# One Strassen level in the output and the down projection of a decoder layer, token parts through DRAM

## The chip, the cores and the metric

One core of a Trainium2 chip. The metric is the device time of one launch in microseconds (us), as the median of timed runs. The engines work side by side, each through its own queue in order: PE (TensorE, matmuls; PEld is its weight load), DVE (VectorE, elementwise), ACT (ScalarE, copies and activations), POOL (GpSimd), and SP, from which all DMAs of this kernel are issued (SPq is its queue). Matmuls write PSUM, eight banks of 128 x 512 floats; the rest lies in SBUF, 128 partitions.

## The reference

One decoder layer on x of 512 tokens x 2048 features, all in float32:

```
h = rms(x) * norm_mix_pre                 proj = h @ w_in
y_a = hgrn2(q, f, i, g) @ w_up_a          y_b = fox(q, k, v, f) @ w_up_b
m = sigmoid(g_a) * y_a + sigmoid(g_b) * y_b
x = x + rms(m @ w_o) * norm_mix_post                       # w_o: 2048 x 2048
h = rms(x) * norm_ffn_pre
gate, up = split(h @ w_ffn_in)                             # 2048 x 2*5632
x = x + rms((silu(gate) * up) @ w_ffn_down) * norm_ffn_post  # 5632 x 2048
```

The two products that the change touches are m @ w_o (the output projection, tiles `wo`) and act @ w_ffn_down (the down projection, tiles `dn`).

## The kernel before

**Products in three passes.** Every float32 operand is split into two parts of the type float32r: ACT copies it to that type (the high part), DVE subtracts the copy from the original (the low part). A product is then three matmuls into one bank: low x high, high x low, high x high (`mm3`, `mm3t`). So each weight tile of 128 x 1024 needs one ACT copy (L135) and one DVE subtraction (L136); `make_w` does it for three tiles ahead.

**Stages.** The input projection with both mixers comes first, with features on the partitions and 512 tokens in the free dimension. `merge` (L500) forms the two gates and adds the branches; its last call leaves the 16 tiles of m in SBUF, feature-major. Then m is split, and `rows_product` makes the output projection: tokens are the stationary side (128 of them), weights move through 512 columns at a time. It runs over two halves of 1024 columns. In each half 8 banks hold 4 token tiles x 2 column tiles, and the loop goes over the 16 k tiles:

```
for i in range(n_k - tail):
    w, a = next_w(), lhs(half, ks[i])
    for t in range(NT):
        block(t, a, w, i == 0, i == n_k - 1)
```

In the second half the last TAIL = 4 k tiles are done bank by bank, so that the token tiles are finished one after another. `wo_done` (L676) takes a finished bank: DVE multiplies it with norm_mix_post (L678), ACT squares and sums it (L679); with the last of a token tile the norm follows (sum, POOL's power, `wor`), the residual is added (L688), stored to DRAM (`x1d`), squared again and scaled (L696). `take_h(th)` transposes a half of 256 tokens on PE (`hp`, L724), scales it out of PSUM (L729) and makes the parts that the next stage wants.

**Gate and up projection (`f..p`, L151 to L153).** This stage is already done with one Strassen level in seven products: p1 to p7 with the token parts h11, h12, s1 to s4, h22 (`hx`) and the weights' parts `fia` to `fid`. The first five blocks do p1 and p2 first (NJ0), which need the first token half alone. Its results go to DRAM, `actd`.

**Down projection.** `rows_product` again, over 44 k tiles in each of two column halves; the activations come back from `actd` (256 KB tiles, L866) and are split for each half (L175, L176). `down_done` scales with norm_ffn_post, and with the last of a token tile makes the norm, adds `x1r` (x1 read back) and stores the output (L901, L902).

**Order.** The Tile framework puts the instructions into each engine's queue, by program order and by what it takes to be ready, and sets all waits. `tc.issue_after(loads[-1].ins)` queues DMAs behind the last weight load. A tile's buffer comes free when its last reader is done; the next tile of its tag waits for that.

## Time and profile before

| | us |
|---|---|
| median of 3 timed runs | 2881.95 (2881.37 to 2884.63) |
| the profiled execution | 2883.7 |
| its span, first to last instruction | 2882.0 |
| output projection | 1284.4 to 1465.2 |
| gate and up projection | 1491.8 to 2388 |
| down projection | 2393 to 2873.7 |

The profile is of one execution. The span is what its instructions cover; the 1.7 us beside it lie around them. A row of a view gives an engine's busy time in a stretch; what an engine waited for stands in brackets in a timeline.

### The profile page before, as it was taken

How to read it: one execution, taken by the hardware profiler on the slowest of the kernel's cores; microseconds unless marked ns; L12 is line 12 of the kernel's file. 1: busy time of each engine (PE TensorE's matmuls, PEld its weight loads, DVE VectorE, ACT ScalarE, POOL GpSimd, SP SyncE). 2: the span in 40 equal slices, each digit the busy share in tenths (PEclk: the TensorE clock that was granted, in tenths of full speed). 3: DMA queues.
4: the chain of work that ended last, by engine and by line, in shares of the span. 5: the costliest groups of instructions: out<-in, count | busy, mean ns of one | idle time of the engine just before them, and what ended most of it. 6: DMA issues, size and time to landing. Idle time of an engine off the chain costs nothing.

```text
span 2882.0 us, 39661 instructions
## 1 busy us (share of the span) xinstructions
PE 2829.7 (98%) x16320; PEld 2495.4 (87%) x16320; DVE 1624.4 (56%) x2311; ACT 1079.1 (37%) x1406; POOL 35.0 (1%) x75
## 2 busy tenths in 40 slices
PE   9999999999999999999969999999999999999998
PEld 7788888888888888888869999999999997888887
DVE  4776665333344433352279888888888885334234
ACT  4454544222233342232264444444444443224222
POOL 1000000000000000000000000000000000000000
PEclk9999999999999999999989999999999999999999
DMA  6323333333333333352344434344343438225353
GB/s 161 101 68 88 81 82 84 99 95 95 98 90 88 88 90 97 96 190 95 96 131 138 130 111 128 111 121 118 114 125 110 129 96 288 95 95 171 132 183 114
DMA packets 465143, 332.93 MB, mean 116 GB/s; under 512 B 12809, under 2 KB 422458, under 8 KB 464962
## 3 DMA queue, kind: packets, MB, share of 16 engines
q1 hardware_dynamic: 464962, 330.39, 39.0%
q8 instruction: 128, 2.10, 0.3%
q14 instruction: 53, 0.43, 0.0%
HBM read 310.40 MB, written 19.94 MB: 115 GB/s over the span
## 4 chain that ended last, share of the span: by engine, by line
PE 96%; DVE 2%; ACT 1%; issue 1%; DMA 0%; POOL 0%; SPq 0%; DVEq 0%; POOLq 0%; ACTq 0%
PE dn L157 6%; PE dn L158 6%; PE dn L159 5%; PE b L151 3%; PE b L153 3%; PE b L152 3%; PE p L151 3%; PE p L152 3%; PE p L153 3%; PE ga L153 2%; PE ga L152 2%; PE gb L151 2%; PE gb L153 2%; PE gb L152 2%; PE ga L151 2%; PE wo L157 2%
## 5 line engine op out<-in xcount | busy, mean ns | idle before, releaser
L136 DVE TENSOR_TENSOR wl<-wr,wh 128x1024 fp32r<-128x1024 f32 (+1 forms) x334 | 404.8, 1212 | 528.3 <-ACT wh L135 527.2
L135 ACT ACTIVATE wh<-wr 128x1024 fp32r<-128x1024 f32 (+1 forms) x334 | 349.8, 1048 | 925.9 <-PE dn L159 155.1
L810 DVE TENSOR_TENSOR fl<-fia,fh 128x1024 fp32r<-128x1024 f32 x88 | 107.7, 1224 | 79.3 <-ACT fh L809 79.3
L809 ACT ACTIVATE fh<-fid 128x1024 fp32r<-128x1024 f32 x88 | 93.4, 1062 | 112.4 <-DVE fid L799 33.1
L809 ACT ACTIVATE fh<-fic 128x1024 fp32r<-128x1024 f32 x88 | 93.4, 1062 | 111.1 <-DVE fic L805 102.7
L810 DVE TENSOR_TENSOR fl<-fic,fh 128x1024 fp32r<-128x1024 f32 x88 | 107.8, 1225 | 34.9 <-ACT fh L809 34.7
L809 ACT ACTIVATE fh<-fia 128x1024 fp32r<-128x1024 f32 x88 | 93.4, 1062 | 90.4 <-DVE fia L803 47.6
L810 DVE TENSOR_TENSOR fl<-fid,fh 128x1024 fp32r<-128x1024 f32 x88 | 107.1, 1217 | 3.5 <-ACT fh L809 3.5
L853 ACT ACTIVATE t<-g 128x512 f32<-128x512 f32 x44 | 27.8, 632 | 95.9 <-DVE g L852 95.9
L809 ACT ACTIVATE fh<-fib 128x1024 fp32r<-128x1024 f32 x44 | 46.7, 1061 | 32.3 <-DVE fib L801 28.5
L805 DVE TENSOR_TENSOR fic<-fia,fic 128x1024 f32<-128x1024 f32 x44 | 53.8, 1224 | 1.3
L799 DVE TENSOR_TENSOR fid<-fid,fib 128x1024 f32<-128x1024 f32 x44 | 53.7, 1220 | 0.1
L801 DVE TENSOR_TENSOR fib<-fib,fia 128x1024 f32<-128x1024 f32 x44 | 53.6, 1218 | 0.0
L810 DVE TENSOR_TENSOR fl<-fib,fh 128x1024 fp32r<-128x1024 f32 x44 | 53.6, 1217 | 0.0
L803 DVE TENSOR_TENSOR fia<-fia,fid 128x1024 f32<-128x1024 f32 x44 | 53.5, 1217 | 0.0
L513 DVE TENSOR_TENSOR sga<-ya,sga 128x512 f32<-128x512 f32 x16 | 11.1, 692 | 52.8 <-PE ya L153 52.8
L506 DVE TENSOR_TENSOR sga<-ga,rb 128x512 f32<-128x512 f32 x16 | 11.1, 692 | 52.0 <-PE ga L153 52.0
L513 DVE TENSOR_TENSOR sgb<-yb,sgb 128x512 f32<-128x512 f32 x16 | 11.1, 692 | 47.7 <-PE yb L153 47.7
L724 PE MATMUL hp<-ident,mo 128*128 128x128 f32 x64 | 12.2, 353 | 21.6 <-DVE mo L696 21.6
L724 PEld LDWEIGHTS hp<-ident,mo 128*128 128x128 f32 x64 | 10.0, 183 | 24.3 <-issue 15.7
L855 DVE TENSOR_TENSOR g<-g,u 128x512 f32<-128x512 f32 x44 | 30.1, 684 | 0.0
L854 DVE TENSOR_TENSOR g<-g,t 128x512 f32<-128x512 f32 x44 | 30.1, 684 | 0.0
(8848 smaller groups left out, 9493.0 us busy)
## 6 DMA issues: line engine op xcount, KB each, us to landing
wr<-in_w_in_dram SPq DMA_DIRECT2D x166, 512.0 KB, 3.9
wr<-in_w_ffn_down_dram SPq DMA_DIRECT2D x88, 512.0 KB, 3.9
fic<-in_w_ffn_in_dram SPq DMA_DIRECT2D x49, 512.0 KB, 4.0
fia<-in_w_ffn_in_dram SPq DMA_DIRECT2D x49, 512.0 KB, 3.9
fid<-in_w_ffn_in_dram SPq DMA_DIRECT2D x44, 512.0 KB, 5.1
fib<-in_w_ffn_in_dram SPq DMA_DIRECT2D x44, 512.0 KB, 4.0
act<-actd SPq DMA_DIRECT2D x88, 256.0 KB, 5.9
wr<-in_w_o_dram SPq DMA_DIRECT2D x32, 512.0 KB, 3.8
```

The costliest lines, as they stand in the source:

```text
L135: hi = nc.scalar.activation(wh[:, 0:width], raw[:, 0:width], AF.Copy)
L136: lo = nc.vector.tensor_tensor(wl[:, 0:width], raw[:, 0:width], wh[:, 0:width].bitcast(F32), ALU.subtract)
L151: nc.tensor.matmul(ps, lhsT=wh, rhs=xl, start=first, stop=False)
L152: nc.tensor.matmul(ps, lhsT=wh, rhs=xh, start=False, stop=False)
L153: nc.tensor.matmul(ps, lhsT=wl, rhs=xh, start=False, stop=last)
L157: nc.tensor.matmul(ps, lhsT=xl, rhs=wh, start=first, stop=False)
L158: nc.tensor.matmul(ps, lhsT=xh, rhs=wl, start=False, stop=False)
L159: nc.tensor.matmul(ps, lhsT=xh, rhs=wh, start=False, stop=last)
L799: nc.vector.tensor_tensor(d, d, b, ALU.subtract)
L805: nc.vector.tensor_tensor(c, a, c, ALU.subtract)
L809: nc.scalar.activation(wh, src, AF.Copy)
L810: nc.vector.tensor_tensor(wl, src, wh.bitcast(F32), ALU.subtract)
```

## The change

Both products are done with one Strassen level (the Winograd form, seven products of half size). K is halved by pairing the k tiles 2i and 2i+1, the columns by pairing 512 with the next 512 (`g` counts such pairs), the tokens into 0 to 255 (f) and 256 to 511 (s). Tokens stay stationary. In its parts:

- `token_parts` makes the sums of the token side, where the pair of tiles is formed, and stores the seven parts of 256 tokens (order XPART) in 1792 columns of DRAM: `md` for m, `actd` for the activations. The former splits of m are gone.
- `Rows` makes a product as a list of items. An A item loads two weight pieces and four token parts and serves p1, p6, p7, p5 (8 banks, 24 matmuls); it also stores the weight sum t2. A B item serves p2, p3, p4 (6 banks, 18 matmuls) and reads t2 back. In the output projection t2 stays in SBUF; there a C item serves p2 and p3 of both column pairs (8 banks, 24 matmuls) and an E item p4 of both (4 banks, 12 matmuls), which is all that token tiles 2 and 3 still lack at that point.
- Order: output projection A (g 0), A (g 1), C, E, 8 items each; down projection A, B (g 0), A, B (g 1), 22 items each. Loads are issued three items ahead, splits two; the last 2 (in the last pass 3) items of a pass are done bank by bank, and `take` adds the products up in SBUF and calls `wo_done` or `down_done`.
- The first half of `take_h(0, i)` comes between E items. xr of tokens 0 to 255 is loaded in the second A pass, the rest after token tiles 0 and 1 are done; x1r in the second A pass of the down projection.
- Buffers: 16 of 128 x 1024 (`wide`) in the place of 32 of 128 x 512; weight parts share 10 (`wpart`). The last block of the gate and up projection does p1 and p2 first.
- `down_done` now squares a sum in SBUF, after the product with norm_ffn_post for every bank.

```diff
-NX = 32
+NX = 16
 NRAW = 3
-NHALF = 5
+NHALF = 10
 AHEAD = 3
 LOAD_AHEAD = 9
 XAHEAD = 2
 GATE_AHEAD = 5
-TAIL = 4
+TAIL_A = 2
+TAIL_B = 3
+LOAD_ITEMS = 3
+LHS_AHEAD = 2
...
+    XPART = {"p5": 0, "p7": 1, "p1": 2, "p6": 3, "p3": 4, "p2": 5, "p4": 6}
+    def token_parts(dst, i, x1, x2):
+        f, s = slice(0, 256), slice(256, 512)
+        sa, sb = big(f"sa{i}"), big(f"sb{i}")
+        nc.vector.tensor_tensor(sa[:, f], x1[:, s], x2[:, s], ALU.add)
+        nc.vector.tensor_tensor(sa[:, s], x1[:, f], x1[:, s], ALU.subtract)
+        nc.vector.tensor_tensor(sb[:, f], sa[:, f], x1[:, f], ALU.subtract)
+        nc.vector.tensor_tensor(sb[:, s], x2[:, f], sb[:, f], ALU.subtract)
+        rows = dst[i * P : (i + 1) * P, :]
+        nc.sync.dma_start(rows[:, 512:768], x1[:, f])
+        nc.sync.dma_start(rows[:, 1280:1792], x2)
+        nc.sync.dma_start(rows[:, 0:512], sa)
+        nc.sync.dma_start(rows[:, 768:1280], sb)
...
+        def load(self, n):
+            kind, g, i = self.items[n]
+            nm = f"{self.name}{n}"
+            rows = self.parts[i * P : (i + 1) * P, :]
+            if kind == "E":
+                x = top["rawx"].tile([P, 1024], F32R, tag="wrawx", name=nm + "x")
+                loads.append(nc.sync.dma_start(x[:, 512:768].bitcast(F32), rows[:, 1536:1792]))
+                self.raw[n] = (x,)
+                return
+            r = wp.tile([P, 1024], F32, tag="wraw", name=nm + "r")
+            d = None
+            if kind == "C":
+                d = wp.tile([P, 1024], F32, tag="wraw", name=nm + "d")
+                nc.sync.dma_start(r, self.piece(2 * i + 1, 0, 1024))
+                nc.sync.dma_start(d, self.piece(2 * i + 1, 1024, 1024))
+            elif kind == "A":
+                d = top["rawx"].tile([P, 1024], F32, tag="wrawx", name=nm + "d")
+                nc.sync.dma_start(d[:, 0:512], self.piece(2 * i + 1, g * 1024 + 512, 512))
+                nc.sync.dma_start(r, self.piece(2 * i, g * 1024, 1024))
+            else:
+                d = top["rawx"].tile([P, 1024], F32, tag="wrawx", name=nm + "d")
+                nc.sync.dma_start(r, self.piece(2 * i + 1, g * 1024, 1024))
+                nc.sync.dma_start(d[:, 0:512], self.t2[i][:, g * 512 : (g + 1) * 512])
+            x = wide(nm + "x")
+            c0, c1 = {"A": (0, 1024), "B": (1024, 1792), "C": (1024, 1536)}[kind]
+            loads.append(nc.sync.dma_start(x[:, 0 : c1 - c0], rows[:, c0:c1]))
+            self.raw[n] = (r, d, x)
...
+            if kind == "A":
+                sub(d[:, f], d[:, f], r[:, s])
+                sub(r[:, s], r[:, s], r[:, f])
+                nc.vector.tensor_tensor(d[:, s], r[:, f], d[:, f], ALU.add)
+                rh, rl, r_lo = parts_of_w(r, "r")
+                dh, dl, d_lo = parts_of_w(d, "d")
+                sub(xl, x[:, 0:width], xh.bitcast(F32))
+                r_lo()
+                d_lo()
+                if self.keep_t2:
+                    if g == 0:
+                        self.t2[i] = wide(f"{self.name}t{i}")
+                    nc.sync.dma_start(self.t2[i][:, g * 512 : (g + 1) * 512], d[:, s])
+                else:
+                    if g == 0:
+                        self.t2[i] = dramp.tile([P, 1024], F32, name=f"{self.name}t{i}")
+                    nc.sync.dma_start(self.t2[i][:, g * 512 : (g + 1) * 512], d[:, s])
+                w = {("p1", g): (rh[:, f], rl[:, f]), ("p5", g): (rh[:, s], rl[:, s]),
+                     ("p7", g): (dh[:, f], dl[:, f]), ("p6", g): (dh[:, s], dl[:, s])}
+            elif kind == "B":
+                rh, rl, r_lo = parts_of_w(r, "r")
+                sub(d[:, f], d[:, f], r[:, f])
+                both = wpart(f"{nm}d")
+                nc.scalar.activation(both[:, f], d[:, f], AF.Copy)
+                sub(xl, x[:, 0:width], xh.bitcast(F32))
+                r_lo()
+                sub(both[:, s], d[:, f], both[:, f].bitcast(F32))
+                w = {("p2", g): (rh[:, f], rl[:, f]), ("p3", g): (rh[:, s], rl[:, s]),
+                     ("p4", g): (both[:, f], both[:, s])}
+            else:
+                t = self.t2[i]
+                for q, src in enumerate((r, d)):
+                    h, l, lo_ = parts_of_w(src, "rd"[q])
+                    if q == 0:
+                        sub(xl, x[:, 0:width], xh.bitcast(F32))
+                    lo_()
+                    sub(t[:, q * 512 : (q + 1) * 512], t[:, q * 512 : (q + 1) * 512], src[:, f])
+                    w["p2", q], w["p3", q] = (h[:, f], l[:, f]), (h[:, s], l[:, s])
+            self.ready[n] = (w, {p: (xh[:, q * 256 : (q + 1) * 256], xl[:, q * 256 : (q + 1) * 256])
+                                 for q, p in enumerate(names)})
...
+        def run(self, n0, n1, order, tail, tail_order, hook=None):
+            banks = {(p, g, t): bank(f"{self.name}{n0}_{p}{g}{t}") for p, g in order for t in range(2)}
+            for n in range(n0, n1 - tail):
+                self.load_to(n + LOAD_ITEMS)
+                self.split_to(n + LHS_AHEAD)
+                for p, g in order:
+                    for t in range(2):
+                        self.block(banks[p, g, t], n, p, g, t, n == n0, False)
+                if hook is not None:
+                    hook(n)
+                del self.ready[n]
+            self.split_to(n1)
+            for at, (p, g, t) in enumerate(tail_order):
+                for n in range(n1 - tail, n1):
+                    self.block(banks[p, g, t], n, p, g, t, n == n0, n == n1 - 1)
+                self.take(p, g, t, banks[p, g, t])
+                if at == 1:
+                    self.load_to(n1 + 2)
+                    self.split_to(n1 + 1)
+            for n in range(n1 - tail, n1):
+                del self.ready[n]
+        def take(self, p, g, t, ps):
+            a, nm = self.acc, f"{self.name}{g}{t}"
+            add = lambda o, u, v: nc.vector.tensor_tensor(o, u, v, ALU.add)
+            if p == "p1":
+                a["c11", g, t] = big(nm + "c11")
+                nc.scalar.activation(a["c11", g, t], ps, AF.Copy)
+            elif p == "p6":
+                a["c12", g, t] = big(nm + "c12")
+                add(a["c12", g, t], ps, a["c11", g, t])
+            elif p == "p7":
+                a["c21", g, t] = big(nm + "c21")
+                add(a["c21", g, t], ps, a["c12", g, t])
+            elif p == "p5":
+                c22 = big(nm + "c22")
+                add(c22, ps, a["c21", g, t])
+                add(a["c12", g, t], ps, a["c12", g, t])
+                self.done(2 + t, 2 * g + 1, c22)
+            elif p == "p2":
+                c11 = a.pop(("c11", g, t))
+                add(c11, ps, c11)
+                self.done(t, 2 * g, c11)
+            elif p == "p3":
+                c12 = a.pop(("c12", g, t))
+                add(c12, ps, c12)
+                self.done(t, 2 * g + 1, c12)
+            else:
+                c21 = a.pop(("c21", g, t))
+                nc.vector.tensor_tensor(c21, c21, ps, ALU.subtract)
+                self.done(2 + t, 2 * g, c21)
...
+        A_ORDER = ("p1", "p6", "p7", "p5")
+        B_ORDER = ("p2", "p3", "p4")
+        def pass_a(self, n0, n1, g, hook=None):
+            self.run(n0, n1, [(p, g) for p in self.A_ORDER], TAIL_A,
+                     [(p, g, t) for p in self.A_ORDER for t in range(2)], hook)
...
+    wo_items = [("A", g, i) for g in range(2) for i in range(KD // 2)]
+    wo_items += [(kind, 0, i) for kind in "CE" for i in range(KD // 2)]
+    wo = Rows("wo", w_o, md, wo_items, lambda *a: wo_done(*a), True)
+    def last_hook(nn):
+        if nn == KD + 1:
+            top["ctx"].close()
+            top["ctx"] = ExitStack()
+            top["rawx"] = top["ctx"].enter_context(tc.tile_pool(name="rawx", bufs=NRAWX, reuse_waits="tile"))
+        if nn == KD + GATE_AHEAD - 1:
+            wo.load_to(2)
+            wo.split_to(1)
+    merge(ob, "b", ma, lambda i, x1, x2: token_parts(md, i, x1, x2), last_hook)
...
+    def wo_hook(at):
+        if at == n + 4:
+            with tc.issue_after(loads[-1].ins):
+                load_rows(0)
+                load_rows(1)
+        if at >= 3 * n + 4:
+            for i in range(2 * (at - 3 * n - 4), 2 * (at - 3 * n - 3)):
+                take_h(0, i)
+    wo.pass_a(0, n, 0)
+    wo.pass_a(n, 2 * n, 1, wo_hook)
+    wo.run(2 * n, 3 * n, [(p, g) for g in range(2) for p in ("p2", "p3")], TAIL_A,
+           [(p, g, t) for t in range(2) for g in range(2) for p in ("p2", "p3")])
+    wo.run(3 * n, 4 * n, [("p4", g) for g in range(2)], TAIL_A, [("p4", g, t) for t in range(2) for g in range(2)],
+           wo_hook)
+    for i in range(2 * (n - TAIL_A - 4), KH):
+        take_h(0, i)
+    for i in range(KH):
+        take_h(1, i)
...
+    apart = list(range(NJ0)) + [KF - 1]
+    work = [(j, p, EARLY) for j in range(NJ0) for p in EARLY]
+    work += [(j, p, REST) for j in range(NJ0) for p in REST]
+    work += [(j, p, ALL) for j in range(NJ0, KF - 1) for p in ALL]
+    work += [(KF - 1, p, EARLY) for p in EARLY] + [(KF - 1, p, REST) for p in REST]
...
+    def down_hook(at):
+        if at == 4:
+            with tc.issue_after(loads[-1].ins):
+                for half in range(2):
+                    r = wide(f"wfp{half}")
+                    nc.sync.dma_start(r, norm_ffn_post[0:1, half * 1024 : (half + 1) * 1024].to_broadcast([P, 1024]))
+                    wfp.extend((r[:, 0:S], r[:, S : 2 * S]))
+        if at >= 2 * nk and (at - 2 * nk) % 4 == 2 and len(x1r) < 16:
+            t = len(x1r) // 4
             with tc.issue_after(loads[-1].ins):
                 for c in range(4):
                     x1r[t, c] = big(f"x1r{t}_{c}")
                     nc.sync.dma_start(x1r[t, c], x1d[t * P : (t + 1) * P, c * S : (c + 1) * S])
...
-            nc.vector.tensor_tensor(mw[t, c], ps, wfp[c], ALU.mult)
-            if c < 2:
-                nc.scalar.activation(ps, ps, AF.Square, accum_out=sst[:, t, c : c + 1])
+        nc.vector.tensor_tensor(mw[t, c], ps, wfp[c], ALU.mult)
+        nc.scalar.activation(ps, ps, AF.Square, accum_out=sst[:, t, c : c + 1])
+        if any((t, c_) not in mw for c_ in range(4)):
             return
...
+    dn = Rows("dn", w_ffn_down, actd, [(kind, g, i) for g in range(2) for kind in "AB" for i in range(nk)],
+              down_done, False)
+    dn.pass_a(0, nk, 0, down_hook)
+    dn.run(nk, 2 * nk, [(p, 0) for p in dn.B_ORDER], TAIL_A, [(p, 0, t) for p in dn.B_ORDER for t in range(2)])
+    dn.pass_a(2 * nk, 3 * nk, 1, down_hook)
+    dn.run(3 * nk, 4 * nk, [(p, 1) for p in dn.B_ORDER], TAIL_B,
+           [("p2", 1, 0), ("p3", 1, 0), ("p2", 1, 1), ("p3", 1, 1), ("p4", 1, 0), ("p4", 1, 1)])
```

## Rows read from the trace of the kernel before

**Rows 1.** the profile's page: busy us of the engines, share of the span, instructions

```profile
PE 2829.7 (98%) x16320; PEld 2495.4 (87%) x16320; DVE 1624.4 (56%) x2311; ACT 1079.1 (37%) x1406; POOL 35.0 (1%) x75
```

**Rows 2.** busy time by stretch: us, busy (instructions) per engine, clock, DMA share, GB/s

```profile
1284.40:1465.20 180.80, 178.74 (x800) 146.99 (x800) 56.97 (x71) 49.81 (x85) 2.19 (x4) 1.00 0.30 97
1465.20:1491.80 26.60, 7.02 (x34) 6.62 (x33) 21.03 (x43) 17.45 (x44) 2.19 (x4) 0.56 0.50 158
1600.00:2300.00 700.00, 700.00 (x5836) 700.00 (x5835) 577.17 (x696) 302.52 (x348) 0.00 (x0) 1.00 0.40 118
2633.00:2873.70 240.70, 240.70 (x1063) 198.98 (x1061) 92.90 (x112) 75.71 (x108) 1.62 (x3) 1.00 0.47 158
2873.70:2882.00 8.30, 0.02 (x1) 0.00 (x0) 3.65 (x7) 0.69 (x2) 0.54 (x1) 0.76 0.49 166
```

**Rows 3.** the same, instructions of the tiles wo and dn alone

```profile
1284.40:1465.30 180.90, 175.91 (x768) 143.73 (x768) 7.71 (x12) 7.85 (x24) 1.00 0.30 97
2393.00:2873.80 480.80, 480.72 (x2112) 397.56 (x2112) 9.75 (x15) 9.95 (x31) 1.00 0.45 151
```

**Rows 4.** timeline of PE, ten matmuls apart: start, us, engine, line, out<-in

```profile
2629.67 0.39 PE L158 MATMUL dn<-wl,as_43h 128*128 128x512 f32 x1
...
2631.94 0.39 PE L159 MATMUL dn<-wh,as_43h 128*128 128x512 f32 x1
```

**Rows 5.** timeline of DVE in the gate and up projection, nothing idle between

```profile
2028.31 0.68 DVE L855 TENSOR_TENSOR g<-g,u 128x512 f32<-128x512 f32 x1
2028.91 1.22 DVE L810 TENSOR_TENSOR fl<-fid,fh 128x1024 fp32r<-128x1024 f32 x1
2030.05 1.22 DVE L810 TENSOR_TENSOR fl<-fib,fh 128x1024 fp32r<-128x1024 f32 x1
```

**Rows 6.** the page's groups: mean ns of one; idle before and what ended it

```profile
L809 ACT ACTIVATE fh<-fid 128x1024 fp32r<-128x1024 f32 x88 | 93.4, 1062 | 112.4 <-DVE fid L799 33.1
```

**Rows 7.** the page's DMA issues: KB each, us to landing

```profile
wr<-in_w_ffn_down_dram SPq DMA_DIRECT2D x88, 512.0 KB, 3.9
act<-actd SPq DMA_DIRECT2D x88, 256.0 KB, 5.9
```

**Rows 8.** busy time by stretch, where the DMA engines were fullest

```profile
2425.00:2445.00 20.00, 20.00 (x90) 16.57 (x89) 6.45 (x7) 6.20 (x8) 0.00 (x0) 1.00 0.98 343
```

**Rows 9.** timeline of PE from the output projection to the gate projection

```profile
1464.76 0.47 PE L159 MATMUL wo<-wh,m15h 128*128 128x512 f32 x1
1480.67 1.94 PE L724 MATMUL hp<-ident,mo 128*128 128x128 f32 x8 [15.44 <-DVE mo L696]
1486.76 5.38 PE L724 MATMUL hp<-ident,mo 128*128 128x128 f32 x24 [4.14 <-DVE mo L696]
1491.79 0.53 PE L151 MATMUL f0p<-hh110l,fh 128*128 128x256 f32 x1
```

**Rows 10.** timeline of PE: starts of the output and of the down projection

```profile
1284.42 0.47 PE L157 MATMUL wo<-wh,m0l 128*128 128x512 f32 x1 [0.88 <-DVE sgb L513]
...
2393.00 0.79 PE L157 MATMUL dn<-wh,as_0l 128*128 128x512 f32 x1 [5.06 <-DVE as_0l L176]
```

**Rows 11.** timeline of DVE after the last matmul, at 2873.7

```profile
2874.48 0.16 DVE L896 TENSOR_REDUCE fs<-sst 128x1 f32<-128x4 f32 x1 [1.10 <-ACT jk L889]
...
2875.49 2.74 DVE L901 SCALAR_TENSOR_TENSOR mw<-mw,fr,x1r 128x512 f32<-128x512 f32 x4
```

**Rows 12.** timeline of PE early in the gate projection, short waits

```profile
1525.72 0.38 PE L151 MATMUL f0p<-hs,fh 128*128 128x256 f32 x1 [1.69 <-DVE hs L714]
...
1527.19 0.58 PE L153 MATMUL f0p<-hs10h,fl 128*128 128x256 f32 x1 [0.85 <-DVE fl L810]
```

**Rows 13.** busy time by stretch, at the lower clock

```profile
1526.00:1536.50 10.50, 8.72 (x39) 7.95 (x39) 8.65 (x15) 5.03 (x10) 0.00 (x0) 0.51 0.35 101
2393.00:2396.70 3.70, 3.70 (x9) 2.93 (x10) 2.95 (x5) 1.83 (x3) 0.00 (x0) 0.50 0.84 288
```

More of the change, by code (lines that the diff above doesn't have):

```diff
@@ L679, in wo_done @@
         nc.scalar.activation(ps, ps, AF.Square, accum_out=so_[:, t, c : c + 1])
-        if c < 3:
+        if any((t, c_) not in mo for c_ in range(4)):
             return
@@ L747, in block_kernel @@
-    rows_product(lambda half, k: ms[k], list(range(KD)), "wo", wo_done)
-    top["ctx"].close()
-    top["ctx"] = ExitStack()
-    rawx = top["ctx"].enter_context(tc.tile_pool(name="rawx", bufs=NRAWX, reuse_waits="tile"))
-    actd = dramp.tile([DFF, S], F32, name="actd")
-    WITH = {"p1": "h11", "p2": "h12", "p3": "s4", "p4": "h22", "p5": "s1", "p6": "s2", "p7": "s3"}
-    work = [(j, p) for j in range(NJ0) for p in ("p1", "p2")]
-    work += [(j, p) for j in range(NJ0) for p in ("p3", "p7", "p5", "p6", "p4")]
```

254 lines of the change are left out of this document (134 added, 120 removed).

## The prediction

> **What bounds the kernel now.** I read the page first. TensorE (PE) is busy for 98% of the span, every other engine far less [rows 1]; the reader should not stop there, because that is a mean over stages. The second view cuts the span by stage [rows 2]. In the output projection PE works for 178.7 of 180.8 us and VectorE (DVE) for 57; in the second half of the down projection PE works for all of 240.7 us and DVE for 93. Between the output projection and the gate projection lie 26.6 us in which PE works for 7 only, and after the last matmul come 8.3 us more. The gate and up projection, which the change touches at its edges alone, already runs DVE at 577 of 700 us without holding PE up. So in both changed stages PE is the limit, with much room on the others, and a matmul taken away is time taken away until another engine becomes as slow as PE. The third view counts what is there to take: 768 matmuls of 512 columns in wo and 2112 in dn [rows 3]. Durations in the timeline overlap, so I take the pace instead: ten matmuls in 2631.94 - 2629.67 = 2.27 us, 0.227 us each [rows 4]; 2112 of these are 479.4 us, and dn took 480.7.
>
> **What is removed.** Seven products of half-size blocks replace eight. Output projection: 8 pairs of k x 7 products x 2 column halves x 2 token tiles x 3 passes = 672 matmuls, 96 fewer. Down projection: 22 x 7 x 2 x 2 x 3 = 1848, 264 fewer. Width and stationary size (128 tokens) stay, so the pace should stay: 360 x 0.227 = **-81.7 us**. The rest is what feeding them costs.
>
> **The feed, DVE.** On dense stretches a 128x512 operation starts the next one 0.60 us later and a 128x1024 one 1.14 us later [rows 5]. An A item (four products) has three sums of 512 and three low parts of 1024: 3 x 0.60 + 3 x 1.14 = 5.22 us, against 24 x 0.227 = 5.45 us of PE. A B item (three products): 1.14 + 0.60 + 0.60 + 0.87 (768 columns, between the two) = 3.21 against 18 x 0.227 = 4.09. A C item 4.08 against 5.45, an E item 1.5 against 2.72. In the down projection that is 44 x 5.22 + 44 x 3.21 = 371 us, plus 44 operations of 512 in take and down_done, 26 us, plus 11 for the last row sums: 408 us beside 419.5 us of PE. DVE goes from less than half busy to 97%. It still fits, but an A pass lets DVE win back only 0.23 us an item, so whatever makes it late stays for a long time. ScalarE has three copies of 1024 in an A item, 1.06 us each [rows 6], 3.2 of 5.45: not a limit.
>
> **The feed, DMA.** Today a load of 512 KB lands 3.9 us after its issue [rows 7]. An A item moves 512 + 256 + 512 KB in and 256 KB of t2 out, 1.57 MB in 5.45 us, 289 GB/s; a B item 1.18 MB in 4.09 us, 288. The fullest 20 us of the trace moved 343 GB/s at a share of 0.98 [rows 8], beside PE at full speed. So the queues run at 84% all through the down projection, with raw buffers for three items. What comes on top is queued in front of weights: xr for tokens 0 to 255 in the second A pass of the output projection (2.1 MB, 6 us of the queue at 343), and x1r in the second A pass of the down projection (4 times 1.05 MB, 3 us each). By the code a load is issued some 7 to 9 us ahead of its split and needs 5 to 6; so I charge 3 us for xr (0 to 6) and 4 for x1r (0 to 15: nothing hidden at all would be 12, and some delay beside).
>
> **Hand-overs between passes.** Here the PSUM banks and DVE's order count. *Merge to the first A pass*: DVE's last two merge operations, token_parts (four sums of 256 columns, about 0.35 each) and the second split come after one another: 1.2 + 1.4 + 5.2 = 7.8 us, while item 0 gives PE 5.45; +2.5 us over today's 0.88 us gap [rows 10] (0 to 5). *A to A*, where no cheap pass lies between: ten operations of 0.60 and two splits, 16.5 us, beside 10.9 us of tail and the next item's 5.45; +3 (0 to 6), because the split also waits for parts that the tail still reads. *C and E*: eight sums, eight products with wpost and two norm chains on DVE, about 19 us, beside 10.9 of tail and the first E items; +5 (0 to 10). *A to B* twice: one short split, 9.2 us in 10.9; +0.5 each. *B to A*: split 5.2 and evictions 7.2 beside 8.2 us of tail, and only then the second item's split, whose first usable part is ready about 10 us after the tail, when PE has had 6 us of work: +4.5 (0 to 9). token_parts in the gate and up projection adds four sums for each two of 44 blocks, 0.7 us to a block, where DVE is idle for 17% of the time [rows 2]: nothing, and up to +8 if that idle time can't be used. Its writes, 0.9 MB where 0.5 went, lie in a stage with 118 GB/s: nothing.
>
> **Between the output and the gate projection.** Today PE is without its own work from 1465.23 to 1491.79, 26.6 us: 15.4 and 4.1 us waiting on mo, and 32 transposes [rows 9]. In the change the first token half is normed during the E pass, and only one product of the second half is left. But DVE, which is busy for 21 of these 26.6 us [rows 2], still has to form two more sums and do both norm chains, and half of take_h(0) is left as well. I take -3 us (-9, the low parts that leave; +6, if the E pass leaves DVE late).
>
> **Start of the down projection and the end.** Today PE waits 5.06 us for the first activations [rows 10]. The new first item needs a 5.2 us split in the place of two operations; some of it fits before the gap; the early p1 and p2 of the last block free buffers. I take +2 (-4 to +8). At the end today 0.16 us of sum, then four 0.685 us operations follow the square [rows 11]; now a sum and the product with wfp, 1.2 us, come before the square, and the token tile before ends only 2 us earlier, so its four operations stand in the way for about 1 us: +2 (1 to 5).
>
> **The clock.** Around two short waits, 1.69 and 0.85 us, the granted clock falls, and from 1526.0 on it is 0.51 over 10.5 us (1.2 GHz in the place of 2.4) [rows 12, 13]; such a spell costs about 5 us if PE is the limit in it. The restart at 2393 ran 3.7 us at 0.50 and cost 1.85. I charge three spells at 4 us for the new hand-overs: +12 (0 to 40). Here the Trainium skill speaks against the change: its page "TensorE: Matmul & The Clock Gate", section "A second HAM failure mode: psum-queue depth-cycling", tells of a kernel that cycled through PSUM banks, idled for moments between groups of matmuls, and had its clock swing between the two levels. By that rule the A passes, where PE and DVE are within 0.23 us an item, could swing throughout. Rows 12 and 13 agree in that the clock fell beside short waits; that the swing keeps up, no row shows.
>
> **Sum.** -81.7 + 2.5 + 3 + 5 + 1 + 4.5 + 3 + 4 - 3 + 2 + 12 + 2 = **-45.7 us**. The profiled execution took 2883.7 us (span 2882.0 and 1.7 around it): 2838.0. It was 1.75 us over the median of the three timed runs, so I forecast **2836 us**. All lower ends together give about -94, all upper ends about +40 (2922).
>
> **The rivals.** *All of it hidden* (0.25). For it: DVE and DMA both fit on paper, and the gate projection runs at 82% of DVE without a wait. Against it: 97%. Only the start (2.5), the end (2), the first down item (2) and one spell (4) are left: -71, 2811 us. *The feed becomes the bound in the A passes* (0.15): in each item one copy of ScalarE, 1.06 us, can't be laid beside DVE's work, as fh waits for DVE already today, 33 us in all [rows 6]. An A item then takes 5.22 + 1.06 = 6.28 us instead of 5.45: 60 x 0.83 = 50 us, which replaces the 15.5 us of hand-overs and loads in the A passes (3 + 1 + 4.5 + 3 + 4): -11, 2871 us; with loads that fall behind as well, no change. *Slower, by the clock* (0.14): PE is held up a little in every A item, the clock falls, and in the spell PE itself is the limit, so DVE's small lead can't heal it. The place is the 60 A items. Without the clock's 12 us the sum is -57.7, so from 12 spells of 5 us on the change loses; at 20 spells (200 of the 327 us of A passes) it is +42, 2924 us. For it: rows 12 and 13. Against it: the dense stretches at 2.4 GHz around them, and that a bounded feed keeps PE at 95% busy. *That less is removed than it says* is not open: the loops fix the counts, and only the pace could differ.
>
> **Chances and range.** The forecast (2820 to 2856) has 0.46, the hidden case 0.25, the bound feed 0.15, the clock 0.14. A measurement here tells about 0.2%, 5.8 us, from no change. Of the bound feed 0.02 lies within it; of the clock case 0.02 within and 0.12 above. So faster 0.84, same 0.04, slower 0.12. The range takes in the forecast, most of the hidden case and half of the bound feed: 2802 to 2872; the likeliest case alone has 2820 to 2856.
>
> **What would show it.** Right: 672 and 1848 matmuls at 0.227 us; the down projection in 425 to 450 us, DVE over 90% busy in it; PE waits of 3 to 6 us at the B to A hand-over; the gap before the gate projection between 18 and 30 us; two to four new stretches at half clock. Wrong: PE waits spread over the A items and ended by DVE or by DMA (bound feed); clock well below 0.95 in the A passes (the clock case); no wait at the hand-overs (all hidden); or a gate and up projection more than 5 us longer, for then token_parts isn't free.

## The result and the profile after

The changed kernel takes **2841.4 us** (three runs, 2840.6 to 2842.2) against 2882.2 us: a ratio of 0.9856, 95% interval 0.9837 to 0.9875. A fourth timed run took 9306.1 us at a mean granted clock of 0.41, where the three have 0.99; it is left out, and its cause is not known. The forecast was 2836, its range 2802 to 2872. The profiled execution has a span of 2840.5 us, 41.5 less than before; every stage below is of the two profiled executions.

First the page's line of busy time. PE is still the fullest engine [rows 1], and DVE has gone from 56% to 70%:

```profile
PE 2764.0 (97%) x15960; PEld 2429.6 (86%) x15960; DVE 1992.7 (70%) x2855; ACT 1209.3 (43%) x1542; POOL 36.5 (1%) x75
```

The windows by stage, columns as in [rows 2]: output projection, what lies between it and the gate projection, a steady piece of the gate and up projection, the whole down projection, and what follows the last matmul:

```profile
1286.60:1465.30 178.70, 164.88 (x690) 130.99 (x691) 151.10 (x204) 90.91 (x137) 3.06 (x4) 0.96 0.68 220
1465.30:1484.80 19.50, 8.58 (x49) 7.65 (x47) 17.15 (x37) 15.92 (x39) 2.81 (x4) 0.65 0.60 189
1600.00:2300.00 700.00, 700.00 (x5835) 700.00 (x5835) 606.76 (x768) 299.70 (x348) 0.00 (x0) 1.00 0.43 129
2379.40:2824.50 445.10, 429.71 (x1850) 348.60 (x1849) 401.25 (x491) 244.78 (x290) 0.54 (x1) 0.99 0.81 277
2824.50:2840.50 16.00, 0.00 (x0) 0.00 (x0) 11.14 (x22) 2.06 (x6) 1.59 (x3) 0.64 0.63 210
```

PE is now idle for 14 to 15 us inside each of the two changed stages, where before it was hardly ever idle. The same for the product tiles alone shows the counts of the change, 672 and 1848, against 768 and 2112 [rows 3]:

```profile
1286.60:1465.30 178.70, 162.86 (x672) 128.73 (x672) 17.12 (x27) 2.38 (x4) 0.96 0.68 220
2379.30:2824.50 445.20, 429.66 (x1848) 348.67 (x1848) 17.73 (x27) 2.25 (x4) 0.99 0.81 277
```

To see where the time went I split each stage by the starts of its matmuls: 0.227 us for each (0.2265 to 0.2267 before rounding) is the base; what lies between two starts beyond that counts as "half clock" inside a stretch at the lower clock (up to 0.2 us a matmul), and as "wait" otherwise.

| us | before | after |
|---|---|---|
| gap ahead of the output projection | 0.88 | 2.75 |
| output projection: base / waits / half clock / transposes | 174.0 / 3.0 / 0 / 3.4 | 152.2 / 17.3 / 5.0 / 3.8 |
| on to the gate projection | 26.6 | 19.5 |
| gate and up projection | 896.1 | 894.9 |
| gap ahead of the down projection | 5.06 | none |
| down projection: base / waits / half clock | 478.8 / 0 / 1.7 | 418.9 / 21.2 / 4.5 |
| after the last matmul | 8.3 | 16.0 |

The base falls by 21.8 + 59.9 = 81.7 us. Of the output projection's 21.8 nothing is left: its waits, its clock and the later start take 14.3 + 5.0 + 0.4 + 1.9. The down projection keeps 35.7 of 59.9. Two gaps win 7.1 and 5.2, and the end gives 7.7 back.

The three waits that answer to [rows 9], and the starts that answer to [rows 10], in PE's timeline; the down projection now follows with no idle time in front of it:

```profile
1286.65 0.77 PE L160 MATMUL wo_p<-wo0rh,wo0l 128*128 128x512 f32 x1 [2.75 <-DVE sgb L518]
...
1473.38 1.76 PE L932 MATMUL hp<-ident,mo 128*128 128x128 f32 x7 [6.33 <-DVE mo L905]
1478.85 0.47 PE L932 MATMUL hp<-ident,mo 128*128 128x128 f32 x1 [3.71 <-ACT hr L937]
1480.20 4.81 PE L932 MATMUL hp<-ident,mo 128*128 128x128 f32 x24 [0.88 <-DVE mo L905]
...
2379.33 0.28 PE L156 MATMUL f43p<-hs,fl 128*128 128x256 f32 x1
2379.45 0.40 PE L160 MATMUL dn_p<-dn0rh,dn0l 128*128 128x512 f32 x1
```

**How a wait in an A pass comes about.** The waits of the down projection are not only at its hand-overs. One of them, at items 13 and 14, in the timelines of the queue that issues loads (SPq), of ACT, DVE and PE (start, duration, instruction, and in brackets the idle time before it and what ended it):

```profile
2444.57 0.33 SPq L689 DMA_DIRECT2D dn14d<-in_w_ffn_down_dram  x1
2445.00 0.38 SPq L755 DMA_DIRECT2D dnt<-dn12d  x1
2445.47 0.38 SPq L697 DMA_DIRECT2D dn14x<-actd  x1
```

```profile
2445.13 1.04 ACT L738 ACTIVATE dn13h<-dn13x 128x1024 fp32r<-128x1024 f32 x1
2451.16 1.06 ACT L738 ACTIVATE dn14h<-dn14x 128x1024 fp32r<-128x1024 f32 x1 [4.99 <-DMA dn14x<-actd]
2452.12 1.04 ACT L714 ACTIVATE dn13rh<-dn13r 128x1024 fp32r<-128x1024 f32 x1
```

```profile
2448.79 0.68 DVE L710 TENSOR_TENSOR dn13r<-dn13r 128x512 f32<-128x512 f32 x1
...
2450.00 0.68 DVE L710 TENSOR_TENSOR dn14d<-dn14d,dn14r 128x512 f32<-128x512 f32 x1
2452.25 1.23 DVE L710 TENSOR_TENSOR dn14l<-dn14x,dn14h 128x1024 fp32r<-128x1024 f32 x1 [1.56 <-ACT dn14h L738]
2453.39 1.22 DVE L710 TENSOR_TENSOR dn13rl<-dn13r,dn13rh 128x1024 fp32r<-128x1024 f32 x1
```

```profile
2453.21 0.51 PE L160 MATMUL dn_p<-dn13rh,dn13l 128*128 128x512 f32 x1 [0.41 <-ACT dn13rh L714]
2454.66 0.50 PE L161 MATMUL dn_p<-dn13rl,dn13h 128*128 128x512 f32 x1 [0.94 <-DVE dn13rl L710]
```

On ScalarE's queue the copy of item 14's token parts stands ahead of the weight copy of item 13, which PE needs first and whose input DVE had finished by 2449.5. The load dn14x was issued at 2445.47, only 0.7 us before ScalarE was free for the copy, and landed 5.7 us later. It was issued after dn14d, which had waited for a buffer until an earlier store of t2 landed; the queue's own wait:

```profile
SPq L689 <- DMA dnt<-dn11d: 2.8, 1, 2.8
```

ScalarE stands still for 5.0 us, in the last 1.7 of them with ready work behind the one instruction that can't go. (The Trainium skill, page "PSUM — Partial Sum Buffer", section "Engine vs sequencer instructions", says that ScalarE's queue is strictly first in, first out; these 1.7 us agree.) DVE is busy 94% of that pass, so it looks like the limit, but it too is idle here. The experiments had to tell apart DVE's load, the traffic, the buffers and this order.

### The profile page after: what moved, and what is told of

Same layout as the page of the kernel before. It is cut to its first block, busy times and chain, and to the rows that moved or that the text cites. A ratio compares the mean times of both kernels' runs of the same rounds, so it can differ in the third digit from the quotient of the medians.

```text
span 2840.5 us, 40513 instructions
## 1 busy us (share of the span) xinstructions
PE 2764.0 (97%) x15960; PEld 2429.6 (86%) x15960; DVE 1992.7 (70%) x2855; ACT 1209.3 (43%) x1542; POOL 36.5 (1%) x75
## 4 chain that ended last, share of the span: by engine, by line
PE 82%; DVE 8%; DMA 6%; issue 2%; ACT 2%; SPq 0%; POOL 0%; DVEq 0%; POOLq 0%; ACTq 0%
PE dn_p L161 3%; PE b L154 3%; PE b L156 3%; PE b L155 3%; PE dn_p L160 3%; PE dn_p L162 3%; PE p L154 3%; PE p L155 3%; PE p L156 3%; PE ga L155 2%; PE ga L154 2%; PE ga L156 2%; PE gb L154 2%; PE gb L155 2%; PE gb L156 2%
## 5 line engine op out<-in xcount | busy, mean ns | idle before, releaser
L138 ACT ACTIVATE wh<-wr 128x1024 fp32r<-128x1024 f32 (+1 forms) x214 | 223.1, 1043 | 649.2 <-PE b L155 146.4
L139 DVE TENSOR_TENSOR wl<-wr,wh 128x1024 fp32r<-128x1024 f32 (+1 forms) x214 | 257.7, 1205 | 232.1 <-ACT wh L138 232.0
L154 PE MATMUL p<-x,wh 128*128 128x512 f32 x416 | 165.3, 397 | 1.7 <-DVE rb L274 1.7
L156 PE MATMUL p<-x,wl 128*128 128x512 f32 x416 | 164.7, 396 | 0.0
L155 PE MATMUL p<-x,wh 128*128 128x512 f32 x416 | 163.4, 393 | 0.0
L154 PE MATMUL b<-x,wh 128*128 128x512 f32 x384 | 154.0, 401 | 0.0
L156 PE MATMUL b<-x,wl 128*128 128x512 f32 x384 | 150.1, 391 | 0.0
L155 PE MATMUL b<-x,wh 128*128 128x512 f32 x384 | 149.7, 390 | 0.0
L154 PE MATMUL gb<-x,wh 128*128 128x512 f32 x256 | 100.7, 393 | 0.9 <-ACT wh L138 0.9
L154 PE MATMUL ga<-x,wh 128*128 128x512 f32 x256 | 100.4, 392 | 0.0
L156 PE MATMUL ga<-x,wl 128*128 128x512 f32 x256 | 100.0, 391 | 0.0
L156 PE MATMUL gb<-x,wl 128*128 128x512 f32 x256 | 99.7, 390 | 0.0
L155 PE MATMUL ga<-x,wh 128*128 128x512 f32 x256 | 99.7, 390 | 0.0
L155 PE MATMUL gb<-x,wh 128*128 128x512 f32 x256 | 99.6, 389 | 0.0
```

Source lines behind the costliest of these rows:

```text
L138: hi = nc.scalar.activation(wh[:, 0:width], raw[:, 0:width], AF.Copy)
L139: lo = nc.vector.tensor_tensor(wl[:, 0:width], raw[:, 0:width], wh[:, 0:width].bitcast(F32), ALU.subtract)
L154: nc.tensor.matmul(ps, lhsT=wh, rhs=xl, start=first, stop=False)
L155: nc.tensor.matmul(ps, lhsT=wh, rhs=xh, start=False, stop=False)
L156: nc.tensor.matmul(ps, lhsT=wl, rhs=xh, start=False, stop=last)
```

## The experiments

Ratios are to the kernel before, with 95% intervals. One caution for reading them: the output projection, whose code most of them leave alone, took from 173.0 to 180.6 us in their profiles, so differences of a few microseconds between two of them are read in the stage that the edit touches. Even there 2 us say little: the down projection took 443.1 us, with 20.8 us of waits, in the run that edits the output projection alone (445.0 and 21.2 in the changed kernel).

**One part alone: the down projection as before.**

```diff
-    dn = Rows("dn", w_ffn_down, actd, ...)          # and its four passes
+    rows_product(act_split, list(range(KF)), "dn", down_done)   # the form of before
```

> Edit: the down projection alone is put back to the form of before (eight products, activations whole through DRAM, no token_parts in the gate and up projection); output projection, its transition and the order of the last gate and up block stay as changed. Theory (the parts add up, as the stages of the two traces say: output projection and its start 0, transition -7, gate and up projection -1, start of the down projection -5 or nothing): 2868 to 2876. Rival by the terms of the sum as predicted (-21.8 + 2.5 + 3 + 5 + 3 - 3 + 8 for the output projection): about 2879. If the two parts work against each other, it comes out above 2882.

2870.2 us (0.9953, 0.9936 to 0.9970), as the theory has it. So the output projection with its transition is worth 12 us of the 41, most of it between the stages: 7.4 us ahead of the gate projection and 2.1 ahead of the down projection. The other 29 come with the down projection's change; that one on the former output projection was not run. Its down projection took 480.4 us. The gap ahead of it, in PE's timeline:

```profile
2382.43 0.77 PE L161 MATMUL dn<-wh,as 128*128 128x512 f32 x1 [2.94 <-ACT wh L139]
```

**The order of the last gate and up block.**

```diff
-    apart = list(range(NJ0)) + [KF - 1]
+    apart = list(range(NJ0))        # the last block in the order ALL again
```

> The last block of the gate and up projection does its seven products in the order of the others (p2 last but one) again. Theory: the down projection starts without a wait because the early p1 and p2 free the token parts' buffers for the first activations 14 us before the end; undone, a wait of 4 to 8 us at that start comes back, with a spell at the lower clock: 2846 to 2852 us. Rival: the wait of 5.06 us went because norm_ffn_post's load no longer stands ahead of the activations; then the start stays without a wait: 2839 to 2843 us.

2842.7 us (0.9861, 0.9847 to 0.9876), and the gap is back:

```profile
2381.65 0.79 PE L160 MATMUL dn_p<-dn0rh,dn0l 128*128 128x512 f32 x1 [4.25 <-DVE dn0l L710]
```

So the early p1 and p2 of the last block are what removes it. But the total moved by 1 us only. In the stage itself, gap and down projection take 4.25 + 443.8 = 448.0 us in the place of 445.0, so 3 us of the gap stay: the waits of the down projection fell from 21.2 to 18.0. That an earlier start gives the feed less lead would explain it, and is not shown. The rest of the difference lies in the output projection and behind it, which the edit leaves alone.

**The order on ScalarE.** First the token-part copy kept in program order everywhere, then from the third item of a pass on.

```diff
-            nc.scalar.activation(xh, x[:, 0:width], AF.Copy)
+            tc.keep_in_program_order(nc.scalar.activation(xh, x[:, 0:width], AF.Copy))
```

> The activations' high copy of an item (L738) is pinned behind the copies of the item before it on ScalarE; nothing else is edited. Theory, order: in the down projection PE waits 20.8 us, and the longer waits come because ScalarE's queue has the activation copy of item n+1 ahead of the weight copies of item n, and that load lands late; with the order turned, a late load costs nothing to item n. Then the waits in the down projection fall to about half, 8 to 12 us, and the kernel takes 2829 to 2834 us. Rival, bandwidth: the loads as such come too late at 83 to 85% of the DMA engines, the wait only moves to the activation copy itself: 2838 to 2844 us, waits 18 to 22 us.

2858.3 us (0.9914, 0.9897 to 0.9930), slower than either side said. The first split can't go early any more: the gap ahead of the down projection is 7.7 us, the one ahead of the output projection 6.0, and hand-overs wait 2 to 4 us each. Yet between those, from item 3 to item 21 of the first A pass, PE doesn't wait at all. In the second A pass it waits at items 48, 52, 56 and 60, about 10 us in all, each just after a group of x1r loads; these are the longest waits in the view of waits for that pass:

```profile
DVE dn53d L710 <- DMA dn53r<-in_w_ffn_down_dram: 4.4, 1, 4.4
DVE dn49d L710 <- DMA dn49r<-in_w_ffn_down_dram: 4.0, 1, 4.0
DVE dn57d L710 <- DMA dn57r<-in_w_ffn_down_dram: 3.6, 1, 3.6
DVE dn61d L710 <- DMA dn61r<-in_w_ffn_down_dram: 3.5, 1, 3.5
```

```diff
+            if i >= 2:
+                tc.keep_in_program_order(xcopy)
```

> Edit: the activation copy of an item's token parts (xh) is kept in program order from the third item of each pass on, so that on ScalarE it can't be put ahead of the weight copies of the item before; the first two items of a pass stay free. Theory (in the first A pass of the down projection PE waits because ScalarE stands at the copy of the next item's late x load, with a ready weight copy behind it): the 7 us of waits there go as they did with the copy pinned everywhere, and the starts and hand-overs, which that made 11 us worse, stay as they are: 2831 to 2836. Rival (the waits come from the raw buffer that waits for its t2 store to land; the order on ScalarE only names who waits): 2839 to 2843.

2839.5 us (0.9848, 0.9833 to 0.9863): no gain in the total that could be told from none. The down projection starts without a gap as before and is 441.1 us, 3.9 shorter, its waits 18.9. Items 9 to 20 of the first A pass are free of waits, but items 7 and 8 wait 3.7 us, as x7 and x8 are late themselves, and the hand-over at item 21 waits 3.9 us in the place of 1.1.

**Loads that were to crowd the weights.** x1r into the last B pass; xr into the C pass.

```diff
-        if at >= 2 * nk and (at - 2 * nk) % 4 == 2 and len(x1r) < 16:
+        if at >= 3 * nk and (at - 3 * nk) % 4 == 2 and len(x1r) < 16:   # hook given to the last pass
```

> Edit: the sixteen x1r loads (4 MB) go from the second A pass of the down projection into its last B pass; nothing else. Theory (they are queued in front of weights and cost 8 to 10 us of PE waits in the A pass, not the 4 charged; the last B pass, at a DMA share of 0.72, has room for them): 2831 to 2834 us, the waits at items 48, 60, 64 and 65 go, the second B pass stays within 2 us. Rival (the crowding only moves, because a B item moves 288 GB/s as well): 2839 to 2843, new PE waits at items 70 to 82. If the last row operations then wait for x1r, the tail is longer than 17 us.

2840.2 us (0.9853, 0.9839 to 0.9868). My theory fell. The last B pass takes the 4 MB without a wait, but the second A pass still waits 7 to 8 us without them, at every third item or so, and its hand-over at item 65 waits 4.5 us in the place of 1.8. ScalarE's timeline in that pass shows the figure of items 13 and 14 again:

```profile
2617.67 1.06 ACT L738 ACTIVATE dn49h<-dn49x 128x1024 fp32r<-128x1024 f32 x1 [4.00 <-DMA dn49x<-actd]
2618.64 1.04 ACT L714 ACTIVATE dn48rh<-dn48r 128x1024 fp32r<-128x1024 f32 x1
```

The time after the last matmul grows from 16.0 to 17.8 us, the sign named for x1r that comes late; yet DVE's timeline has no wait for x1r there, so the cause of these 1.8 us is open.

```diff
-        if at == n + 4:
+        if at == 2 * n:                # hook given to the C pass
```

> Edit: the loads of xr for tokens 0 to 255 go from the second A pass of the output projection into its C pass. Theory (they make the x parts of items 12 and 15 5 to 7 us late and so cost the 3 us wait at item 15): 2837 to 2839.5, that wait below 1 us. Rival (C's split and evictions are late by it instead, or DVE sets that wait): 2840.5 to 2843.

2840.1 us (0.9853, 0.9838 to 0.9868). The wait at item 15 falls from 3.0 to 1.6 us, but two new ones at item 14 make up for it (8.5 us in that stretch, 8.6 before), and the load of item 15 is late with no xr in front of it:

```profile
ACT wo12h L738 <- DMA wo12x<-md: 6.7, 1, 6.7
ACT wo15h L738 <- DMA wo15x<-md: 5.6, 1, 5.6
```

The way to the gate projection, further on, takes 24.8 us in the place of 19.5, and the gate and up projection, which starts later, 889.5 in the place of 894.9: for the total the two cancel, so neither theory nor rival is decided by it.

**Buffers and traffic.** The second weight combination t2 stored from POOL's queue; every second raw buffer d from the larger pool; no t2 store at all.

```diff
-                    nc.sync.dma_start(self.t2[i][:, g * 512 : (g + 1) * 512], d[:, s])
+                    nc.gpsimd.dma_start(self.t2[i][:, g * 512 : (g + 1) * 512], d[:, s])
```

> The stores of t2 to DRAM go out from POOL's queue in the place of SP's. Theory, order: what holds SP up is the weight sum's buffer d, which comes free only when the store of t2 three items before has landed, not the place of the store in SP's queue; so it changes little: 2837 to 2845 us. Rival, SP's queue: loads stand behind the store, which waits for DVE; with the store gone they go out earlier and the waits in the down projection fall from 20.8 to 10 us or less: 2828 to 2834 us.

2858.4 us (0.9916, 0.9900 to 0.9933), worse than either side said. The down projection is 462.2 us, its waits 31.9. SP stands longer at the buffer that waits for its store to land, up to 6.8 us here; the last line is the longest such wait in the first A pass of the changed kernel:

```profile
SPq L689 <- DMA dnt<-dn3d: 6.8, 1, 6.8
SPq L689 <- DMA dnt<-dn5d: 6.5, 1, 6.5
```

```profile
SPq L689 <- DMA dnt<-dn6d: 3.8, 1, 3.8
```

So that loop, store, buffer, next load, can set the pace.

```diff
+                if not self.keep_t2 and i >= 2 and i % 2 == 0:
+                    d = wide(nm + "d")
```

> Edit: in the down projection every second A item takes its raw buffer for the second weight piece from the pool of token parts (16 tiles) in the place of the pool of three, so that a load need not wait for a store to land; all work and traffic stay. Theory (the buffer, not the traffic): waits in the A passes fall by 6 to 10 us, 2831 to 2836. Rival (DVE or the queue itself): 2838 to 2843. If earlier loads only crowd the token parts, it is slower, to 2850.

2836.8 us (0.9840, 0.9824 to 0.9856). The time is near the theory's, the stage is not: the down projection took 443.8 us with 20.5 us of waits (445.0 and 21.2 before the edit), and the rest came from the output projection, which the edit leaves alone. Inconclusive for the total. In the first A pass PE's waits up to item 18 do fall, from 7 us to 2.2, with the traffic as it was; but items 19 to 21, before the hand-over, wait 7.5 us in the place of 1.1, and the second A pass gains nothing. So the buffer has a part in the waits between the hand-overs, and freeing it for every second item is not enough. The longest of the new waits, at item 21:

```profile
PE dn_p L161 <- DVE dn21rl L713: 2.8, 1, 2.8
```

```diff
-                    nc.sync.dma_start(self.t2[i][:, g * 512 : (g + 1) * 512], d[:, s])
+                    self.t2[i] = self.piece(2 * i, 0, 1024)     # B items load plain weights
```

> Edit, in the down projection only: the second weight combination of an A item is not stored to DRAM, and the B item loads 256 KB of plain weights in its place (so the p4 product is of other data). An A item moves 256 KB less and its raw buffer is free as soon as the copies and low parts have read it. Theory (PE's waits in the A passes come from that buffer: it is freed when the store has landed, the next loads stand behind it on SP, and the x parts land late): the 21 us of waits in the down projection fall to 12 or less, 2828 to 2834 us. Rival (DVE, busy 93% in the A passes, makes the waits): 2838 to 2843, waits still 18 to 22.

2829.5 us (0.9813, 0.9788 to 0.9838; runs from 2823.3 to 2836.6). The waits of the down projection are 12.8 us, a little over the 12 of the theory; the first A pass has none up to item 20. This edit takes away the store, the wait for it and its traffic together, so it does not tell them apart.

**DVE's load.**

```diff
-                sub(xl, x[:, 0:width], xh.bitcast(F32))
+                if self.keep_t2:                # the output projection
+                    sub(xl, x[:, 0:width], xh.bitcast(F32))
+                else:
+                    xl = xh
```

> Edit, in the down projection only: the low part of an A item's token parts is not formed (the high part is used in its place, so the result lacks that term); the matmuls stay 24 to an item. DVE has 1.14 us less to do per A item, 4.08 against PE's 5.45. Theory (DVE's reserve of 0.23 us an item is what turns each late load into a PE wait, since nothing is won back): waits of the down projection fall from 21 to 8 or less, 2826 to 2833. Rival (raw buffers and late x loads make the waits, whatever DVE's load): 2838 to 2843.

2844.4 us (0.9865, 0.9850 to 0.9881): not faster at all, and a little slower than the rival's range, with waits of 24.9 us, 6.4 of them at the hand-over at item 65 (1.8 in the changed kernel). Windows of the two A passes, first of the changed kernel, then of this one; the third number in each row's busy times is DVE:

```profile
2379.40:2496.00 116.60, 111.48 (x478) 89.99 (x478) 109.71 (x134) 60.74 (x62) 0.00 (x0) 0.99 0.82 275
2602.00:2717.00 115.00, 111.49 (x477) 89.77 (x476) 106.73 (x124) 59.49 (x68) 0.00 (x0) 0.99 0.86 299
```

```profile
2379.40:2496.00 116.60, 111.73 (x479) 90.06 (x478) 90.48 (x110) 64.99 (x67) 0.00 (x0) 0.99 0.89 297
2602.00:2717.00 115.00, 108.56 (x460) 86.82 (x460) 82.61 (x100) 58.31 (x63) 0.00 (x0) 0.99 0.84 286
```

DVE went from 94% to 78% in the first A pass, and PE waited about as much; in the second it waited more. DVE's load is not what makes the waits.

**The tail.**

```diff
-           [("p2", 1, 0), ("p3", 1, 0), ("p2", 1, 1), ("p3", 1, 1), ("p4", 1, 0), ("p4", 1, 1)])
+           [("p4", 1, 0), ("p4", 1, 1), ("p2", 1, 0), ("p3", 1, 0), ("p2", 1, 1), ("p3", 1, 1)])
```

> The last pass's tail does p4 of token tiles 2 and 3 first, then p2 and p3 of tiles 0 and 1. Theory: the 16.0 us after the last matmul are DVE's backlog of three token tiles, 12 row operations of 0.66 us and their sums; with p4 first two tiles are done before the end and one and a half remain: 10 to 12 us after the last matmul, the kernel 2836 to 2838 us. Rival: the work on DVE is the same and it has no idle time in the tail, so the end stays within 1.5 us: 2840 to 2843 us.

2836.3 us (0.9841, 0.9826 to 0.9855), 5 us below the changed kernel; but in its profile the time after the last matmul is 15.3 us in the place of 16.0, so 0.7 of it is the tail's, and the rest lies in stages and passes that the edit leaves alone. DVE's timeline at the end, of the changed kernel and of this one:

```profile
2827.73 5.39 DVE L1118 SCALAR_TENSOR_TENSOR mw<-mw,fr,x1r 128x512 f32<-128x512 f32 x8 [0.41 <-POOL fr L197]
...
2834.03 2.74 DVE L1118 SCALAR_TENSOR_TENSOR mw<-mw,fr,x1r 128x512 f32<-128x512 f32 x4 [0.66 <-POOL fr L197]
```

```profile
2825.00 2.74 DVE L1118 SCALAR_TENSOR_TENSOR mw<-mw,fr,x1r 128x512 f32<-128x512 f32 x4 [0.43 <-POOL fr L197]
...
2828.65 2.74 DVE L1118 SCALAR_TENSOR_TENSOR mw<-mw,fr,x1r 128x512 f32<-128x512 f32 x4 [0.66 <-POOL fr L197]
```

The last matmul ends at 2824.5 in the one and 2820.0 in the other: three token tiles' last operations come after it in the first, two in the second. But in front of them stand six operations of 512 columns in the second, four in the first, so most of the gain is given back: DVE's work is the same, as the rival has it.

**A version that beats both.** Token parts asked for one item earlier, the copy in order in the steady part, p4 first in the tail; the first of the three edits:

```diff
+            if not self.keep_t2 and n + 1 < len(self.items) and self.items[n + 1][2] >= 3:
+                self.early_x[n + 1] = self.load_x(n + 1)     # ahead of this item's weight loads
```

> Three edits together, whole computation kept: in the down projection the token parts of an item are asked for one item earlier, so that their load stands ahead of the weight loads that wait for raw buffers; the copy of the token parts stays in program order from the third item of each pass on; and the p4 products of the last pass come first in its tail. Theory (late x loads on ScalarE's queue, caused by traffic and buffers and not by DVE's load, make the waits of the A passes): waits of the down projection fall from 21 to 8 to 14 us, no ScalarE wait for an x load over 3 us in the A passes, and 2825 to 2833 us. Rival (the queues are the limit: an earlier x load makes the weight loads late by as much): waits 17 to 22, ended by r and d loads, 2833 to 2838, the gain of the tail order alone.

**2833.4 us** (2830.2 to 2835.2; 0.9825, 0.9812 to 0.9838), 8 us below the change, at the edge between the theory's range and the rival's. The stage decides for the theory: the down projection is 435.5 us in the place of 445.0, its waits 14.6 (a little over the 14 allowed), and none of ScalarE's longest waits in either A pass is for an x load any more. The first rows of the view of waits for the first A pass, of the changed kernel and of this one ("issue" is no wait that the profile can name):

```profile
ACT dn17h L738 <- DMA dn17x<-actd: 5.3, 1, 5.3
...
ACT dn14h L738 <- DMA dn14x<-actd: 5.0, 1, 5.0
```

```profile
ACT dn3rh L723 <- issue: 4.3, 1, 4.3
ACT dn8rh L723 <- DVE dn8r L719: 4.2, 1, 4.2
```

Windows of the two A passes:

```profile
2379.40:2496.00 116.60, 114.88 (x514) 94.61 (x513) 112.89 (x137) 61.39 (x63) 0.00 (x0) 1.00 0.86 295
2602.00:2717.00 115.00, 107.78 (x461) 86.84 (x460) 103.17 (x118) 58.82 (x60) 0.00 (x0) 0.99 0.87 294
```

In the first, PE's waits up to item 20 are about 0.6 us where they were about 7, with the whole traffic (295 GB/s) and DVE busy at 97%; the hand-over at item 21 adds 1.9, where it was 1.1. So neither the queues nor DVE are the limit up to there; the order of loads and copies was, and with it the buffers that loads in front of the token parts wait for. How much of it the earlier asking does by itself was not run: with the copy in order alone the down projection took 441.1 us. In the second A pass 9.1 us of waits are left up to item 62, the longest at items 48, 53, 58 and 62, and the four groups of x1r loads are in it, one ahead of each. That they are what is left there is likely, also from the run with every copy in order, but this version with the x1r loads moved was not run.

## Why the forecast came out right, step by step

The forecast was 5 us low, 4.2 us on the profile's own scale (-41.5 for -45.7). That it came so close is in part luck: several of its terms were off, together some 20 us in one direction and 17 in the other, and made up for each other.

- **What is removed** was right: 672 and 1848 matmuls at 0.227 us, 81.7 us less base.
- **The feed, DVE.** The sum of 408 us for the down projection was right (401 of 445 us). What I drew from it, that DVE's small reserve lets every delay stay, was wrong: with 1.14 us less per A item nothing got faster, and at 97% DVE kept PE fed.
- **Hand-overs and loads in the down projection** are the step that failed: 1 + 4.5 + 4 = 9.5 us forecast, 21.2 measured. Around the first hand-over from A to B I find some 3.7 us, around the second 4.1 (1 for both was forecast); around the one from B to A 0.6 and then 2.4 at item 48, where 3 to 6 were named as a sign of being right. The rest, some 10 us, is spread over the A items, where I had put nothing but x1r. The cause is a late x load in front of a ready weight copy on ScalarE, which I had set aside as "not a limit" by its busy share. I had the loads issued 7 to 9 us ahead of their split; dn14x was issued 0.7 us before ScalarE was free for its copy, behind loads that had waited for buffers. That this makes the waits is shown for the first A pass up to item 20 (about 7 us, and 0.6 with the earlier load and the copy in order); for the hand-overs and the second A pass it is open what share it has. The x1r term was 4; in the run with every copy in order about 10 us of waits follow those loads, yet moving them alone gained nothing: late x loads were then still there (items 48 and 49 above).
- **Output projection.** Start +2.5 forecast, +1.9 measured. Its hand-overs and xr, 3 + 5 + 3 = 11, came to 14.3 more waits than before; the xr term was wrong in its cause, as the late x loads are there without xr.
- **Transition** -3, measured -7.1, inside its bounds: PE's waits for mo and hr are 10.9 us in the place of 19.6, and DVE is busy for 17 us there, not 21.
- **Start of the down projection** +2, measured -5.2, beyond the lower end of -4: the early p1 and p2 of the last block let the whole first split go ahead.
- **The end** +2, measured +7.7, beyond the upper end of 5. I let one token tile's four operations stand in the way for 1 us. In fact DVE has some 1.2 us to do per eviction and 3 per token tile, 19 us for the six evictions and four tiles, beside 12 us of matmuls in the tail; so twelve operations, 8.1 us, come after the last matmul, where four, 2.7 us, did before.
- **The clock** +12, measured about +8 (5.0 and 2.8 more in the two stages), in six short stretches at half clock where one was before; two to four new ones were forecast. The slower case, in which the clock keeps falling through the A passes, is refuted: the granted clock is 0.99 over the down projection with 21 us of short waits in it. The Trainium skill's section "A second HAM failure mode: psum-queue depth-cycling" (page "TensorE: Matmul & The Clock Gate") tells of such a swing; this trace has single spells and no lasting swing.
- **token_parts at nothing** was right: the gate and up projection is 1.2 us shorter, with DVE at 607 of 700 us.

Of the rivals, "all of it hidden" is refuted by the waits. The bound feed is there in small: not the 0.83 us an item of a ScalarE copy beside DVE, but single waits of 1 to 3 us. One figure in the argument against the clock's rival does not follow: with 6.28 us for an item PE would be busy for 5.45 of them, 87%, not 95%.

## What to carry to other kernels

When a change takes work from the bounding engine, price what the queues in front of it do in order, not only their busy shares: one instruction that waits for a late load holds everything behind it. Issue the load that the first instruction of an item needs ahead of loads that wait for buffers; here that, with the copies kept in order, made the down projection 9.5 us shorter. And sum the last evictions on their own engine against the tail's matmuls: what doesn't fit there comes after the end in full.

## What was not expected of the hardware

- The queues carried 295 GB/s at a DMA share of 0.86 over 116.6 us of an A pass, in which PE waited some 2.5 us from end to end: here a share well over 0.8 was no sign of a bound by itself.
- Taking some 20 us of DVE work out of each A pass of the down projection moved nothing, though DVE had been busy for 94% of it.
- A store of 256 KB given to POOL's queue instead of SP's made the down projection 17 us longer (462.2 us for 445.0).
